# A two-layer encoder trunk on one core: the order of wide and narrow matmuls inside each projection

## The chip, the core and the metric

The kernel runs on one core of a Trainium2 chip. The core has five engines that run side by side, each through its own queue in order: TensorE (PE in the profile, with PEld for its weight loads), VectorE (DVE), ScalarE (ACT), GpSimd (POOL) and SyncE (SP), which here only issues DMA transfers. Engines wait for each other through semaphores. The metric is the device time of one execution in microseconds (us); before and after are compared by medians.

## The reference

An encoder of two residual layers over 256 tokens with 2048 features, batch 1, all in float32. Layer 0 mixes tokens by attention, layer 1 by a recurrence; each is followed by a gated feed-forward block with 5632 hidden features.

```
for i in range(2):
    h = rms_norm(x, norm_mix[i])
    mix = attention_mixer(h, ...) if i == 0 else recurrent_mixer(h, ...)
    x = x + mix
    h = rms_norm(x, norm_ffn[i])
    x = x + (silu(h @ w_gate) * (h @ w_up)) @ w_down
```

Attention has 16 query heads and 4 key and value heads of 128 features, a norm on queries and keys, and rotary positions. The recurrence has an input projection into two branches, a convolution of width four, gates, a forward and a backward scan, and an output projection. Almost all arithmetic is in the large projections.

## The kernel before, in words

Activations lie with features on the 128 partitions and the 256 tokens along the free dimension; 2048 features are 16 such tiles. Every large matrix is streamed once, in half chunks of eight (or six) blocks of 128 x 128 for one output tile. `load_half` (L83) fetches a half chunk with one DMA, ScalarE rounds it to the matmul's reduced format (`hi`, L93), and VectorE forms the remainder (`lo`, L94). Raw, hi and lo have five buffers each. The order in which half chunks are fetched is written out in advance (L114 to L121).

Activations are split in the same way: the first 256 columns of an activation tile hold the rounded values and the next 256 the remainders. A product is the sum of hi times both parts and lo times the rounded part; the product of the two remainders is left out. So each block of weights needs two matmuls in `blocks` (L153): hi against all 512 columns (L155), and lo against the first 256 (L156), accumulated into the second half of a PSUM tile `acc` of 512 columns. `evac` (L196) or `add_residual` (L279) later adds the halves of `acc`. There are four `acc` tiles.

`project` (L159) makes one output tile from two half chunks (16 blocks; 14 for some of the down projections). Feed-forward units, queries, values and most output tiles go through it. The keys call `blocks` with groups of four blocks (L329), and `output` (L178) calls it with whole half chunks, the first six blocks of one, and the last two. The recurrent layer's input projection, and the last output tile of each feed-forward block, use `project_sum` (L170) instead: three matmuls of 256 columns for each block, through `three` (L165).

The order of instructions on TensorE is that of the program. Small matmuls of other stages (scores, transposes, gates, norms) are inserted by hand: `later(delay, fn)` puts a stage on a list, and `step()` (L140), called once after every block, counts a clock and runs the oldest stage that is due. On the other engines a scheduler orders the instructions.

Of the kernel before, what the change touches and what calls it, by code (L numbers as in the profile page):

```python
# [19 lines left out]
S = 256  # L20
# [8 lines left out]
HALF = 8  # L29
# [30 lines left out]
def trunk(ctx, tc, w, out):  # L60
    nc = tc.nc
    act, dve, pool, pe, sync = nc.scalar, nc.vector, nc.gpsimd, nc.tensor, nc.sync
# [11 lines left out]
    def nm(s):  # L74
        uid[0] += 1
        return f"{s}_{uid[0]}"
# [47 lines left out]
    def half():  # L124
        n = taken[0]
        taken[0] += 1
        if n == 0:
            return load_half(*order[n], [partial(load_x, 2 * i, 2) for i in range(2)])
        if n < KT // 2 and n % 2 == 0:
            load_x(2 * n, 4)  # L130
        return load_half(*order[n])
# [8 lines left out]
    def step():  # L140
        clock[0] += 1
        due = [i for i, (t, _) in enumerate(waiting) if t <= clock[0]]
        if due:
            waiting.pop(due[0])[1]()
# [5 lines left out]
    def new_acc():  # L150
        return ps_a.tile([P, 2 * S], F32, tag="acc", name=nm("acc"))

    def blocks(acc, wt, xs, k0, total=KT):  # L153
        for k, (hi, lo) in enumerate(wt, k0):
            pe.matmul(acc, hi, xs[k], start=(k == 0), stop=False)  # L155
            pe.matmul(acc[:, S:], lo, xs[k][:, :S], start=False, stop=(k == total - 1))  # L156
            step()

    def project(xs):  # L159
        acc = new_acc()  # L160
        for k0 in range(0, len(xs), HALF):
            blocks(acc, half(), xs, k0, len(xs))
        return acc
# [14 lines left out]
    def output(xs, ready, norm, close):  # L178
        accs = [new_acc() for _ in range(FRONT)]
        for acc in accs:  # L180
            blocks(acc, half(), xs, 0)
        late = [half() for j in range(2)]
        for acc, wt in zip(accs, late):
            blocks(acc, wt[: ready - HALF], xs, HALF)
        flush()
        close()
        for j in range(KT):
            if j < 2:
                blocks(accs[j], late[j][ready - HALF :], xs, ready)
            elif j < FRONT:  # L190
                blocks(accs[j], half(), xs, HALF)
            acc = accs[j] if j < FRONT else project(xs)
            add_residual(j, acc, norm)
        norm.finish_later()
# [131 lines left out]
    for i in range(2 * KT // 4):  # L326
        wt = half()
# [397 lines left out]
```

## Time and profile before

| what | us |
|---|---|
| median of 3 executions | 2116.88 (2115.84 to 2120.38) |
| the profiled execution, its own time | 2129.33 |
| its span, first to last instruction | 2127.6 |
| TensorE busy within the span | 2085.5 |
| VectorE busy | 1502.9 |
| ScalarE busy | 1050.4 |
| GpSimd busy | 473.4 |

Busy times of engines overlap, so they don't add up. Matmuls are pipelined: the row of a matmul lasts from its start to a modelled end, and the next one starts well before that. The granted clock of TensorE averaged 0.993 of full speed. Lines are those of the kernel; one line can serve many places, as L155 and L156 serve all products that go through `blocks`.

### The profile page before, as it was taken

The numbers are of one execution on the slowest core, as the hardware profiler recorded it, in microseconds if no ns is written. First come the engines' busy times: TensorE is split into PE (matmuls) and PEld (weight loads), VectorE is DVE, ScalarE is ACT, GpSimd is POOL, SyncE is SP. The second block draws the span as 40 slices with busy tenths as digits, with TensorE's granted clock in tenths as the row PEclk, the third lists the DMA queues.
The fourth block names the chain that finished last, engine by engine and source line by source line (L and its number), as shares of the span: only waits on it lengthen the run. The fifth ranks groups of instructions, "written<-read, shape, count | busy, mean of one in ns | idle before, by whom it ended". The sixth has DMA issues, their size and how long they took to land.

```text
span 2127.6 us, 32676 instructions
## 1 busy us (share of the span) xinstructions
PE 2085.5 (98%) x12512; PEld 1848.4 (87%) x12512; DVE 1502.9 (71%) x2192; ACT 1050.4 (49%) x1598; POOL 473.4 (22%) x454
## 2 busy tenths in 40 slices
PE   7899999999999999999999998999999999999999
PEld 6788888888888888888999997888888888888888
DVE  8899876666566666668889898866666566666665
ACT  5465544443344434444587877454443444444442
POOL 5564431110011100113345553411110011001100
PEclk9999999999999999999999999999999999999999
DMA  6433655555555555555645454555555555665564
GB/s 239 146 122 118 203 187 189 185 185 186 187 188 188 173 186 195 188 183 177 196 160 169 161 166 157 185 188 190 190 194 189 189 189 187 183 203 190 188 189 138
DMA packets 112045, 384.27 MB, mean 181 GB/s; under 512 B 12560, under 2 KB 14736, under 8 KB 111888
## 3 DMA queue, kind: packets, MB, share of 16 engines
q1 hardware_dynamic: 111744, 382.17, 54.4%
q8 instruction: 98, 1.61, 0.3%
q14 instruction: 59, 0.48, 0.1%
q10 hardware_dynamic: 144, 0.02, 0.0%
HBM read 380.04 MB, written 2.10 MB: 180 GB/s over the span
## 4 chain that ended last, share of the span: by engine, by line
PE 86%; DVE 6%; issue 3%; ACT 2%; DMA 1%; POOL 1%; SPq 0%; ACTq 0%; DVEq 0%; POOLq 0%
PE acc L155 53%; PE acc L156 27%; DVE lo L94 2%; DMA graw<-in_w_gates_dram 1%; PE acc L168 1%; PE acc L167 1%; ACT sg L298 1%; PE acc L166 1%; PE pm L167 1%; POOL hb L351 1%; DVE xc L539 1%; PE pm L168 1%; DVE h L621 1%; ACT hi L93 1%; PE pm L166 1%
## 5 line engine op out<-in xcount | busy, mean ns | idle before, releaser
L94 DVE TENSOR_TENSOR lo<-raw,hi 128x1024 fp32r<-128x1024 f32 (+2 forms) x721 | 901.0, 1250 | 509.0 <-ACT hi L93 495.8
L93 ACT CAST hi<-raw 128x1024 fp32r<-128x1024 f32 (+2 forms) x721 | 740.8, 1029 | 928.2 <-PE acc L155 533.6
L155 PE MATMUL acc<-xg,hi 128*128 128x512 f32 x3200 | 1133.1, 398 | 5.7 <-ACT hi L93 5.7
L156 PE MATMUL acc<-xg,lo 128*128 128x256 f32 x3200 | 900.7, 281 | 5.4 <-DVE lo L94 5.4
L155 PEld LDWEIGHTS acc<-xg,hi 128*128 128x128 f32 x3200 | 603.4, 189 | 144.3 <-ACT hi L93 5.7
L155 PE MATMUL acc<-act,hi 128*128 128x512 f32 x1892 | 664.9, 396 | 4.6 <-DVE act L204 4.6
L156 PEld LDWEIGHTS acc<-xg,lo 128*128 128x128 f32 x3200 | 607.8, 190 | 7.1 <-DVE lo L94 7.0
L156 PE MATMUL acc<-act,lo 128*128 128x256 f32 x1892 | 530.9, 281 | 0.4 <-DVE lo L94 0.4
L155 PEld LDWEIGHTS acc<-act,hi 128*128 128x128 f32 x1892 | 355.8, 188 | 87.8 <-DVE act L204 5.5
L497 POOL TENSOR_TENSOR fg<-fg,nr 128x256 f32<-128x256 f32 x88 | 126.1, 1433 | 1189.9 <-ACT fg L298 1189.9
L156 PEld LDWEIGHTS acc<-act,lo 128*128 128x128 f32 x1892 | 358.4, 189 | 0.7 <-DVE lo L94 0.7
L168 PE MATMUL acc<-xg,lo 128*128 128x256 f32 x512 | 146.0, 285 | 3.0 <-DVE lo L94 3.0
L166 PE MATMUL acc<-xg,hi 128*128 128x256 f32 x512 | 146.4, 286 | 2.2 <-ACT hi L93 2.2
L167 PE MATMUL acc<-xg,hi 128*128 128x256 f32 x512 | 145.9, 285 | 0.0
L168 PEld LDWEIGHTS acc<-xg,lo 128*128 128x128 f32 x512 | 99.2, 194 | 3.8 <-DVE lo L94 3.8
L166 PEld LDWEIGHTS acc<-xg,hi 128*128 128x128 f32 x512 | 99.2, 194 | 3.1 <-ACT hi L93 3.1
L167 PEld LDWEIGHTS acc<-xg,hi 128*128 128x128 f32 x512 | 99.1, 194 | 0.0
L280 DVE TENSOR_TENSOR x<-x,acc 128x256 f32<-128x256 f32 x126 | 52.9, 420 | 57.8 <-PE acc L156 57.8
L254 POOL TENSOR_TENSOR ss<-ss,sq 128x256 f32<-128x256 f32 x60 | 78.1, 1302 | 4.9 <-ACT sq L250 0.7
L252 POOL TENSOR_TENSOR sq<-x 128x256 f32<-128x256 f32 x45 | 34.6, 769 | 114.6 <-DVE x L281 112.6
L244 DVE SCALAR_TENSOR_TENSOR xg<-x,pk,xg 128x256 fp32r<-128x256 f32 x64 | 56.2, 891 | 5.2 <-POOL xg L243 5.2
L351 POOL TENSOR_TENSOR hb<-hy,rope 32x256 f32<-32x256 f32 x60 | 46.1, 769 | 44.7 <-DVE hv L419 37.9
(164 smaller groups left out, 1486.6 us busy)
## 6 DMA issues: line engine op xcount, KB each, us to landing
raw<-in_w_gate_dram SPq DMA_DIRECT2D x176, 512.0 KB, 3.6
raw<-in_w_up_dram SPq DMA_DIRECT2D x176, 512.0 KB, 3.6
raw<-in_w_down_dram SPq DMA_DIRECT2D x128, 512.0 KB, 3.6
raw<-in_w_in_dram SPq DMA_DIRECT2D x64, 512.0 KB, 4.0
raw<-in_w_down_dram SPq DMA_DIRECT2D x64, 384.0 KB, 3.1
raw<-in_w_qv_dram SPq DMA_DIRECT2D x40, 512.0 KB, 3.7
raw<-in_w_o_dram SPq DMA_DIRECT2D x32, 512.0 KB, 3.6
raw<-in_w_out_dram SPq DMA_DIRECT2D x32, 512.0 KB, 3.7
```

Source lines behind the costliest of these rows:

```text
L93: act.copy(hi[:, sl, :], raw[:, sl, :])
L94: dve.tensor_tensor(lo[:, sl, :], raw[:, sl, :], hi[:, sl, :].bitcast(F32), ALU.subtract)
L155: pe.matmul(acc, hi, xs[k], start=(k == 0), stop=False)
L156: pe.matmul(acc[:, S:], lo, xs[k][:, :S], start=False, stop=(k == total - 1))
L166: pe.matmul(o, hi, x[:, :S], start=start, stop=False)
L167: pe.matmul(o, hi, x[:, S:], start=False, stop=False)
L168: pe.matmul(o, lo, x[:, :S], start=False, stop=stop)
L244: dve.scalar_tensor_tensor(t[:, S:], x_sb[k], g, t[:, :S].bitcast(F32), ALU.mult, ALU.subtract)
L254: pool.tensor_tensor(self.ss, self.ss, sq, ALU.add)
L280: dve.tensor_tensor(x_sb[j], x_sb[j], acc[:, :S], ALU.add)
L351: eng.tensor_tensor(b[32 * j : 32 * j + 32], y[32 * i : 32 * i + 32], s[32 * i : 32 * i + 32], ALU.mult)
L497: pool.tensor_tensor(g, g, norm.r, ALU.mult)
```

## The change

Within each call of `blocks`, the matmuls of 512 columns are no longer alternated with those of 256. All hi matmuls of the call are issued in a run, and all lo matmuls in another. Usually the hi run comes first. A call is turned, lo run first, if it is a later part of a product (`k0 >= HALF`), has more than four blocks, and the call before it was not turned. For a product of two half chunks this gives eight matmuls of 512, sixteen of 256 and eight of 512, and the next product begins with 512 again. `step()` is still called once per block: behind two of every three hi matmuls and one of every three lo matmuls. `stop` is set on whichever matmul is the last of its product. `three` and `project_sum` are as before.

```
-        for k, (hi, lo) in enumerate(wt, k0):
-            pe.matmul(acc, hi, xs[k], start=(k == 0), stop=False)
-            pe.matmul(acc[:, S:], lo, xs[k][:, :S], start=False, stop=(k == total - 1))
-            step()
+        def rounded():
+            for k, (hi, _) in enumerate(wt, k0):
+                pe.matmul(acc, hi, xs[k], start=(k == 0), stop=(k == total - 1 and turned))
+                if (k - k0) % 3 != 2:
+                    step()
+
+        def rest():
+            for k, (_, lo) in enumerate(wt, k0):
+                pe.matmul(acc[:, S:], lo, xs[k][:, :S], start=False, stop=(k == total - 1 and not turned))
+                if (k - k0) % 3 == 2:
+                    step()
+
+        turned = k0 >= HALF and narrow[0] and len(wt) > HALF // 2
+        narrow[0] = not turned
+        for part in (rest, rounded) if turned else (rounded, rest):
+            part()
```

More of the change, by code (lines that the diff above doesn't have):

```diff
@@ L151, in new_acc @@
         return ps_a.tile([P, 2 * S], F32, tag="acc", name=nm("acc"))
+    narrow = [True]
     def blocks(acc, wt, xs, k0, total=KT):
-        for k, (hi, lo) in enumerate(wt, k0):
-            pe.matmul(acc, hi, xs[k], start=(k == 0), stop=False)
-            pe.matmul(acc[:, S:], lo, xs[k][:, :S], start=False, stop=(k == total - 1))
-            step()
+        def rounded():
[12 more added lines that the diff above has]
+            part()
     def project(xs):
```

## The prediction

> **What bounds the kernel now.** I read the page first. TensorE is busy nearly all the time and carries the chain that ended last; two lines make up four fifths of that chain.
>
> ```profile
> span 2127.6 us, 32676 instructions
> PE 2085.5 (98%) x12512; PEld 1848.4 (87%) x12512; DVE 1502.9 (71%) x2192; ACT 1050.4 (49%) x1598; POOL 473.4 (22%) x454
> PE 86%; DVE 6%; issue 3%; ACT 2%; DMA 1%; POOL 1%; SPq 0%; ACTq 0%; DVEq 0%; POOLq 0%
> ...
> L155 PE MATMUL acc<-xg,hi 128*128 128x512 f32 x3200 | 1133.1, 398 | 5.7 <-ACT hi L93 5.7
> L156 PE MATMUL acc<-xg,lo 128*128 128x256 f32 x3200 | 900.7, 281 | 5.4 <-DVE lo L94 5.4
> ...
> L155 PE MATMUL acc<-act,hi 128*128 128x512 f32 x1892 | 664.9, 396 | 4.6 <-DVE act L204 4.6
> ...
> L156 PE MATMUL acc<-act,lo 128*128 128x256 f32 x1892 | 530.9, 281 | 0.4 <-DVE lo L94 0.4
> ```
>
> The change touches 3200 + 1892 = 5092 pairs of one 512-column and one 256-column matmul, and nothing else. The mean durations in these rows (398 and 281 ns) are no price: matmuls overlap, and what counts is the distance between starts. The idle time in front of the four groups is 16.1 us in all, so weights and activations are almost always there in time. So the question is what a pair costs when TensorE runs without a wait, and whether that price depends on the order.
>
> The price comes from the view by stretches, restricted to line 155, over two long stretches of feed-forward work, one in each layer.
>
> ```profile
> core 0: us, PE busy (x) PEld busy (x), PEclk, DMA share, GB/s
> 300.00:960.00 660.00, 659.20 (x1867) 350.57 (x1866) 1.00 0.56 186
> 1400.00:2050.00 650.00, 650.00 (x1876) 350.62 (x1875) 1.00 0.57 189
> ```
>
> Both stretches are full and at full granted clock, yet a pair takes 660.00/1867 = 353.5 ns in the first and 650.00/1876 = 346.5 ns in the second. The same code runs in two rhythms that differ by 7.0 ns a pair, and 1867 pairs at the slower one are 13.1 us of this execution. Weighted, the two stretches give 1310/3743 = 350.0 ns.
>
> The timeline shows how a pair divides in the fast rhythm:
>
> ```profile
> 1500.02 0.39 PE L155 MATMUL acc<-xg,hi 128*128 128x512 f32 x1
> 1500.25 0.28 PE L156 MATMUL acc<-xg,lo 128*128 128x256 f32 x1
> 1500.37 0.39 PE L155 MATMUL acc<-xg,hi 128*128 128x512 f32 x1
> 1500.60 0.28 PE L156 MATMUL acc<-xg,lo 128*128 128x256 f32 x1
> ```
>
> 0.23 us pass from a 512 to the 256 behind it, 0.12 us from a 256 to the 512. The recurrent layer gives the one neighbour that the change needs and that exists today, a 256 behind a 256 with a weight load before each:
>
> ```profile
> 1149.80 0.28 PE L167 MATMUL acc<-xg,hi 128*128 128x256 f32 x1
> 1149.92 0.28 PE L168 MATMUL acc<-xg,lo 128*128 128x256 f32 x1
> 1150.04 0.28 PE L166 MATMUL acc<-xg,hi 128*128 128x256 f32 x1
> ...
> 1150.64 0.28 PE L168 MATMUL acc<-xg,lo 128*128 128x256 f32 x1
> ```
>
> From 1149.80 to 1150.64 there are seven steps, so one is 120 ns. If a matmul's price depends on its own width alone, the 512 costs 346.5 - 120 = 226.5 ns. The difference of 106.5 ns for 256 columns is 0.416 ns a column, and both widths then leave the same rest: 120 - 106.5 = 13.5 ns, and 226.5 - 213.0 = 13.5 ns. That is what I take from the rows: a column price plus a fixed turn of 13.5 ns for each matmul with its weight load, whoever the neighbour is. It is an inference, since two prices always fit a line, but it asks for no cost of changing the width.
>
> **The change part by part.** It removes, adds and resizes no instruction. For each half chunk it issues eight 512s and eight 256s in runs; second halves of more than four blocks are turned, so that 256s meet 256s in the middle of a product and 512s meet 512s between products.
>
> First, the 256 behind a 256. It replaces the 0.12 us step that a 256 costs today; with the row of 120 ns and the division above this is 0 ns a pair.
>
> Second, the 512 behind a 512. No row of this trace has one. Its ends from the nearest rows are 213.0 ns (the column price with no turn at all) and 233.5 ns (the slow rhythm's pair of 353.5 less 120). I take 226.5, the fast rhythm's value, because the stretches of pure 256s show the turn of 13.5 ns without any change of width. In a stretch that is fast now that is a change of 0.
>
> At this term a rule of the Trainium skill speaks otherwise. TensorE: Matmul & The Clock Gate, section "Back-to-back issue gap", gives N/2.4 + 2.5 ns at full clock for an isolated stream; by it, as an estimate, a pair is 215.8 + 109.2 = 325 ns. This trace does not agree for alternating pairs (346.5) nor for pure 256s (120); whether it holds for a run of 512s no row shows.
>
> Third, the slow rhythm. Its steps are strictly regular, and its weight is 13.1 us in the first stretch. It appears only in the alternation of widths, and the order that carries it is gone. Whether runs of 512s have a slow rhythm of their own, and whether the unprofiled executions spend as long in it, no row tells: the gain lies between 0 and 13.1 us. I take the middle, 6.5 us. The profiled execution took 2129.33 us (span 2127.6 and 1.7 around it), 12.45 above the median of 2116.88; that distance could be this rhythm or the recording.
>
> Fourth, waits for weights. In a plain half only the rounded part is needed at first, and the remainder 8 x 226.5 = 1.81 us later. Such waits exist almost only at the beginning:
>
> ```profile
> 14.10 0.40 PE L155 MATMUL acc<-xg,hi 128*128 128x512 f32 x1
> 16.78 0.58 PE L156 MATMUL acc<-xg,lo 128*128 128x256 f32 x1 [2.29 <-DVE lo L94]
> ...
> 26.44 0.39 PE L155 MATMUL acc<-xg,hi 128*128 128x512 f32 x1
> 29.46 0.39 PE L156 MATMUL acc<-xg,lo 128*128 128x256 f32 x1 [2.63 <-DVE lo L94]
> ```
>
> At 26.44 seven more 512s (1.6 us) could run while TensorE waits for the remainder; at 14.10, in a group of four, three (0.7 us). The second wait lasts longer if the first is left earlier, so 1.6 us is the upper end. What is late next is the attention's chain over VectorE and GpSimd:
>
> ```profile
> PE pm L166 <- DVE qs L203: 4.7, 1, 4.7
> ...
> POOL hb L351 <- DVE hv L419: 37.9, 13, 5.6
> ```
>
> The scores wait 4.7 us for qs, later than both places, and that chain would swallow a head start. Between 0 and 1.6 I take 0.6 us. The lower end is not below nothing: no operand is needed earlier than now, except that a turned half wants its remainder 0.23 us sooner.
>
> Fifth, buffers. In a plain half the rounded weights are given back after 1.81 instead of about 2.65 us; in a turned half the remainders after 8 x 120 = 0.96 us. Only earlier, never later.
>
> ```profile
> ACT hi L93 <- PE acc L155: 533.6, 337, 3.7
> ...
> DVE lo L94 <- ACT hi L93: 495.8, 389, 4.6
> ```
>
> ScalarE waits 533.6 us for such a release, that is, the weights are already cast as far ahead as buffers allow. Earlier casts and the loads behind them collide with nothing on the chain. 0 us.
>
> Sixth, the steps that trigger the delayed stages. Eight calls a half stay eight, six in the run of 512s and two in that of 256s. In a plain half the sixth now comes after 1.81 instead of 2.08 us, 0.27 early; in a turned half the third comes after 0.96 + 0.23 = 1.19 instead of 1.04, 0.15 late. A stage that is inserted early makes TensorE stand in order behind its wait, with all later projections queued behind it. The 4.7 us wait could grow by 0.27, and a shift could remove or add a drop of the granted clock. I put this at 0, with 2 us to either side.
>
> The sum against the profiled execution is 2129.3 - 6.5 - 0.6 = 2122.2 us; the same 7.1 us from the median give 2109.8, so the forecast is **2110 us**. With the ends of the rhythm and the 2 us it reaches from 2101 to 2118.
>
> **The rivals.** *Runs of 512s are cheaper.* The turn may be a cost of the change of width rather than of each matmul. Against it stands the pure 256 stretch, which has no change of width and still pays 120. For it: there the weight load may be what fills the 120 ns, which says nothing about a 512. 512s meet 512s in 15 of 16 cases, 4774 times. With the whole turn gone this gives 4774 x 13.5 = 64 us, so 2052; with half of it gone, 32 us, so 2085. Chance 0.17. By the skill's rule (TensorE: Matmul & The Clock Gate, "Back-to-back issue gap") a 512 would be 215.8 ns, 51 us less and about 2066; the trace so far speaks against that rule for both widths that it shows.
>
> *Runs of 512s settle in the slow rhythm: slower.* In the slow stretch it is the pair with a 512 that lengthens, while the stretches of pure 256s hold 120. If a 512 behind a 512 takes 233.5 ns everywhere, a pair is 353.5 against 350.0 now: 5092 x 3.5 = 18 us more, 2135; if the unprofiled executions now run wholly in the fast rhythm, 5092 x 7.0 = 36 us, 2153. It decides from a pair above 350.8 ns on, where 0.8 ns x 5092 pass 4.2 us. Speaking against it: the slow rhythm is not met in every stretch today. Chance 0.24.
>
> *The order does not matter at all.* The share of each rhythm stays, or the unprofiled executions are fast already, and the beginning is swallowed by the attention's chain: 2116 to 2118. For it speaks that sum and count of instructions are the same. Chance 0.17.
>
> **How the numbers follow.** The forecast has the remaining 0.42. About 0.2% (4.2 us) can be told from no change. Of the forecast's case, from 2101 to 2118, 0.27 lie below 2112.7 and 0.15 above. Faster: 0.27 + 0.17 = 0.44. Same: 0.15 + 0.15 of the third rival = 0.30. Slower: 0.24 + 0.02 = 0.26. The range takes half of the first rival's span and half of the second's: 2085 to 2136, leaving out about 0.09 at each end. The likeliest case's own range is 2101 to 2118.
>
> **What would show it.** In the timeline of the second feed-forward block: 512 to 512 near 226 ns, 256 to 256 near 120 ns; 213 to 220 proves the first rival, 233 or more the second. In the two stretches: 346 to 347 ns a pair in both proves the third term, 353 in either one refutes it. In the first 30 us: the waits for the remainders shrink by about 1.6 us together, and the wait for qs grows by as much. A group of line 204 or 94 that suddenly holds TensorE for tens of microseconds, or more half-clock stretches in the attention, would make the prediction wrong for a reason that it does not name.

## The result, and the profile after

The changed kernel takes 2131.51 us (median of 4, 2128.63 to 2133.55) against 2117.71 us before (4 executions, three of them those shown above, 2115.84 to 2120.38): a ratio of 1.0063, with a 95% interval from 1.0046 to 1.0081. It is slower by 0.6%. Yet the two profiled executions are of the same length, 2127.6 us before and 2126.8 us after. Both facts have to be explained.

The page after shows TensorE with 12 us less busy time in the same span, and a chain that runs less over TensorE (81% against 86%) and more over VectorE and ScalarE:

```profile
PE 2073.5 (97%) x12512; PEld 1850.8 (87%) x12512; DVE 1519.5 (71%) x2192; ACT 1056.1 (50%) x1598; POOL 477.5 (22%) x454
...
PE 81%; DVE 9%; issue 3%; ACT 3%; POOL 2%; DMA 1%; SPq 0%; ACTq 0%; DVEq 0%; POOLq 0%
```

First the feed-forward work. Line 155 has become line 160, line 156 line 166. The view by stretches for line 160, with the same two stretches as before:

```profile
300.00:960.00 660.00, 451.94 (x1894) 347.96 (x1895) 1.00 0.58 188
1400.00:2050.00 650.00, 445.81 (x1869) 343.03 (x1868) 1.00 0.58 188
```

A pair takes 660.00/1894 = 348.5 ns in the first stretch and 650.00/1869 = 347.8 ns in the second. The slow rhythm of the first stretch (353.5) is gone, and the second (346.5) is 1.3 ns a pair dearer. The timeline shows the new order, eight 512s, sixteen 256s, and then 512s of two products:

```profile
1499.81 1.98 PE L160 MATMUL acc<-xg,hi 128*128 128x512 f32 x8
1501.63 2.08 PE L166 MATMUL acc<-xg,lo 128*128 128x256 f32 x16
1503.54 2.68 PE L160 MATMUL acc<-xg,hi 128*128 128x512 f32 x11
```

The last row is cut off by the end of the view.

Eight steps from 1499.81 to 1501.63 are 227.5 ns for a 512; sixteen from 1501.63 to 1503.54 are 119 ns for a 256. So far this is what was forecast, and worth 1894 x 5.0 = 9.5 us less in the first stretch and 1869 x 1.3 = 2.4 us more in the second.

What came back against it lies in the attention. The view by stretches from 100 to 200 us, before and then after; the counts are matmuls, weight loads, and instructions of VectorE, ScalarE and GpSimd:

```profile
100.00:200.00 100.00, 99.02 (x612) 85.61 (x611) 97.11 (x219) 61.23 (x185) 63.76 (x73) 1.00 0.38 127
```

```profile
100.00:200.00 100.00, 86.19 (x539) 73.05 (x538) 88.29 (x194) 53.38 (x164) 65.36 (x66) 1.00 0.32 111
```

TensorE starts 539 matmuls instead of 612. Before, VectorE was busy 97.11 of these 100 us and TensorE 99.02: here VectorE had almost no slack, although the page shows it at 71% of the whole span. After, VectorE and TensorE both have gaps. The wait view after names a wait that did not exist before, for the normalised softmax weights:

```profile
PE pm L454 <- DVE pr L448: 14.6, 24, 1.9
```

The copies of a head's projection out of PSUM mark the heads (first and last start in the stretch), before and after:

```profile
L198 ACT COPY hy<-acc x12: 358/364/371, 101.5 to 191.7; 128x256 f32<-128x256 f32 x12
```

```profile
L214 ACT COPY hy<-acc x10: 372/372/373, 109.0 to 191.7; 128x256 f32<-128x256 f32 x10
```

A head took 90.2/11 = 8.20 us before and takes 82.7/9 = 9.19 us after.

The two profiles can also be cut where TensorE starts the first 512-column matmul of a stage. The stretch of the sixteen query heads takes 134.0 us before and 146.0 after; the first feed-forward block together with the recurrence behind it 995.4 and 982.2; the second feed-forward block 728.6 and 730.7. So 12.0 us lost in the attention meet 13.2 us gained where the slow rhythm stood, and the two profiles are equally long. That the timed executions before had no slow rhythm to lose follows from the experiments.

Why, the queues of VectorE and ScalarE show. One head on VectorE before, then after (hv, rsq_s and hf work out a head's scale, mx its scaled maximum; pr are the softmax weights, here normalised, and qs is the split query):

```profile
136.97 0.15 DVE L419 SCALAR_TENSOR_TENSOR hv<-ms,ebt 128x2 f32<-128x2 f32 x1
...
137.63 0.32 DVE L274 TENSOR_TENSOR rsq_s<-hv,hf 128x2 f32<-128x2 f32 x1 [0.17 <-ACT hf L298]
...
139.54 0.16 DVE L423 TENSOR_TENSOR mx<-mx,hf 128x2 f32<-128x2 f32 x1
139.65 1.74 DVE L94 TENSOR_TENSOR lo<-raw,hi 128x1024 fp32r<-128x1024 f32 x1
...
142.11 1.12 DVE L432 TENSOR_SCALAR pr<-pr,rs 128x256 f32<-128x256 f32 x2
143.15 0.28 DVE L203 CAST qs<-hq 128x256 fp32r<-128x256 f32 x1
```

```profile
131.33 0.69 DVE L435 SCALAR_TENSOR_TENSOR hv<-ms,ebt 128x2 f32<-128x2 f32 x1
...
133.21 1.49 DVE L94 TENSOR_TENSOR lo<-raw,hi 128x1024 fp32r<-128x1024 f32 x1
134.63 0.69 DVE L290 TENSOR_TENSOR rsq_s<-hv,hf 128x2 f32<-128x2 f32 x1
135.33 0.29 DVE L219 CAST qs<-hq 128x256 fp32r<-128x256 f32 x1
...
136.79 0.15 DVE L439 TENSOR_TENSOR mx<-mx,hf 128x2 f32<-128x2 f32 x1
...
138.41 1.45 DVE L448 TENSOR_SCALAR pr<-pr,rs 128x256 f32<-128x256 f32 x2
```

Before, the remainder of a later half chunk (L94) and the split of the query (qs) stand behind the chain hv, rsq_s, mx; after, they stand inside it. From hv to mx it takes 2.57 us before and 5.46 us after. ScalarE's queue changed in two places. Before, then after:

```profile
139.74 0.56 ACT L298 ACTIVATE pr<-pm,mx,hf 128x256 f32<-128x256 f32 x1 [0.93 <-DVE mx L423]
...
141.89 0.37 ACT L198 COPY hy<-acc 128x256 f32<-128x256 f32 x1
```

```profile
131.19 1.05 ACT L93 CAST hi<-raw 128x1024 fp32r<-128x1024 f32 x1
132.13 0.21 ACT L314 ACTIVATE rsq_s<-hv 128x2 f32<-128x2 f32 x1
...
132.66 0.21 ACT L314 ACTIVATE hf<-rsq_s 128x2 f32<-128x2 f32 x1
136.36 0.37 ACT L214 COPY hy<-acc 128x256 f32<-128x256 f32 x1 [3.50 <-PE acc L160]
136.98 0.56 ACT L314 ACTIVATE pr<-pm,mx,hf 128x256 f32<-128x256 f32 x1 [0.24 <-DVE mx L439]
```

A weight cast runs ahead of rsq_s, and the exponential pr stands behind the copy of the next projection, which waits 3.50 us for TensorE. Before, the exponential stood ahead of that copy. Neither place costs much by itself in this head: rsq_s starts 0.11 us behind the end of hv (132.02), and the copy is over at 136.73, while the exponential waits another 0.24 us for mx; in every other head it starts right behind the copy, about 0.3 us after mx. The long delay is on VectorE: ScalarE's hf is over at 132.87, but VectorE's rsq_s, which needs it, starts at 134.63, as the remainder ahead of it ends. VectorE ran its queue in order here. The Trainium skill says the same (TensorE: Matmul & The Clock Gate, section "Architectural detail: the array is 16× 32×32, not 1× 128×128"): ScalarE and VectorE are strict first-in, first-out queues; these rows agree.

TensorE then waits in its own queue for pr, in the middle of a run, with all later projections behind it:

```profile
136.47 1.64 PE L160 MATMUL acc<-xg,hi 128*128 128x512 f32 x6
139.23 0.30 PE L454 MATMUL pm<-cn,pr 128*128 128x128 f32 x1 [1.12 <-DVE pr L448]
139.91 0.55 PE L454 MATMUL pm<-cn,pr 128*128 128x128 f32 x3 [0.38 <-DVE pr L448]
```

### The profile page after: what moved, and what is told of

Its sections match the earlier page's. It is cut to its first block, busy times and chain, and to the rows that moved or that the text cites. A ratio compares the mean times of both kernels' runs of the same rounds, so it can differ in the third digit from the quotient of the medians.

```text
span 2126.8 us, 32818 instructions
## 1 busy us (share of the span) xinstructions
PE 2073.5 (97%) x12512; PEld 1850.8 (87%) x12512; DVE 1519.5 (71%) x2192; ACT 1056.1 (50%) x1598; POOL 477.5 (22%) x454
## 4 chain that ended last, share of the span: by engine, by line
PE 81%; DVE 9%; issue 3%; ACT 3%; POOL 2%; DMA 1%; SPq 0%; ACTq 0%; DVEq 0%; POOLq 0%
PE acc L160 51%; PE acc L166 27%; DVE lo L94 3%; DMA graw<-in_w_gates_dram 1%; POOL hb L367 1%; ACT sg L314 1%; ACT pr L314 1%; DVE xc L555 1%; DVE h L637 1%; PE acc L182 1%; PE acc L183 1%; PE acc L184 1%; ACT L314 1%; DVE th L632 1%; DVE pr L448 1%
## 5 line engine op out<-in xcount | busy, mean ns | idle before, releaser
L94 DVE TENSOR_TENSOR lo<-raw,hi 128x1024 fp32r<-128x1024 f32 (+2 forms) x721 | 907.6, 1259 | 138.5 <-ACT hi L93 110.6
L93 ACT CAST hi<-raw 128x1024 fp32r<-128x1024 f32 (+2 forms) x721 | 741.3, 1030 | 435.4 <-PE acc L160 353.1
L160 PE MATMUL acc<-xg,hi 128*128 128x512 f32 x3200 | 780.9, 393 | 7.3 <-ACT hi L93 6.8
L160 PE MATMUL acc<-act,hi 128*128 128x512 f32 x1892 | 458.1, 392 | 5.1 <-DVE act L220 5.1
L166 PEld LDWEIGHTS acc<-xg,lo 128*128 128x128 f32 x3200 | 413.4, 192 | 19.7 <-DVE lo L94 4.0
L166 PE MATMUL acc<-xg,lo 128*128 128x256 f32 x3200 | 421.1, 284 | 2.7 <-DVE lo L94 2.7
L160 PEld LDWEIGHTS acc<-act,hi 128*128 128x128 f32 x1892 | 347.4, 189 | 71.4 <-DVE act L220 5.3
L166 PEld LDWEIGHTS acc<-act,lo 128*128 128x128 f32 x1892 | 246.1, 192 | 10.5
L166 PE MATMUL acc<-act,lo 128*128 128x256 f32 x1892 | 249.7, 283 | 0.0
L214 ACT COPY fg<-acc 128x256 f32<-128x256 f32 x88 | 32.9, 374 | 235.0 <-PE acc L160 235.0
L184 PE MATMUL acc<-xg,lo 128*128 128x256 f32 x512 | 145.8, 285 | 2.5 <-DVE lo L94 2.5
L214 ACT COPY fu<-acc 128x256 f32<-128x256 f32 x88 | 32.7, 372 | 231.6 <-PE acc L160 231.6
L182 PE MATMUL acc<-xg,hi 128*128 128x256 f32 x512 | 146.0, 285 | 1.2 <-ACT hi L93 1.2
L215 DVE TENSOR_TENSOR fu<-acc,fu 128x256 f32<-128x256 f32 x88 | 37.3, 424 | 146.4 <-ACT fu L214 146.4
L215 DVE TENSOR_TENSOR fg<-acc,fg 128x256 f32<-128x256 f32 x88 | 37.3, 424 | 134.2 <-ACT fg L214 134.1
L184 PEld LDWEIGHTS acc<-xg,lo 128*128 128x128 f32 x512 | 98.9, 193 | 3.3 <-DVE lo L94 3.3
```

Source lines behind the costliest of these rows:

```text
L93: act.copy(hi[:, sl, :], raw[:, sl, :])
L94: dve.tensor_tensor(lo[:, sl, :], raw[:, sl, :], hi[:, sl, :].bitcast(F32), ALU.subtract)
L160: pe.matmul(acc, hi, xs[k], start=(k == 0), stop=(k == total - 1 and turned))
L182: pe.matmul(o, hi, x[:, :S], start=start, stop=False)
L184: pe.matmul(o, lo, x[:, :S], start=False, stop=stop)
L214: act.copy(t, acc[:, S:])
```

## The experiments

The theories. **A**: the loss sits in the attention and comes from the order of the queues of ScalarE and VectorE. **B**: the kernel before is not always 2118 us long; something other than its rhythm (recording, transfers) makes its profiled execution longer. **C**: runs of 512s are dearer than alternation, everywhere. **D**: in the attention, the places of the inserted stages or the runs themselves make TensorE wait.

**The kernel before, again (e1).** No edit.

> The kernel before, unchanged, run and profiled once more. Theory A (the loss sits in the attention; the profiled execution before was long because of a slow rhythm of the alternating pairs, 353.5 instead of 346.5 ns a pair between 300 and 960 us): its own timed executions stay near 2117 us, and if this profile shows 346.5 ns a pair in both long stretches its span is near 2115 us; if it shows 353.5 in one, near 2127. Theory B (recording makes an execution of this kernel 12 us longer): the profiled execution is again near 2129 whatever the rhythm.

Twelve executions lay between 2114.90 and 2144.02 us, median 2132.36; A had expected them near 2117. All executions of the kernel before that were timed beside the experiments cluster at three levels, and the mix differs from session to session, also between the last two, which ran on the same chip:

| executions of the kernel before | to 2124 us | 2124 to 2136 | above 2136 |
|---|---|---|---|
| beside e1 to e4, 34 | 18 | 13 | 3 |
| beside e5 to e8, 31 | 8 | 12 | 11 |
| beside e9 to e12, 13 | 0 | 3 | 10 |
| beside e13 to e15, 25 | 23 | 2 | 0 |
| all, with 19 others, 122 | 55 | 36 | 31 |
| median of the level, us | 2118.5 | 2131.2 | 2142.5 |

Three single executions of it were profiled besides, for the other levels (e9, e10, e11).

> The kernel before once more, for one profiled execution. Executions so far lie at three levels, about 2118, 2131 and 2142 us. Rhythm theory: a pair takes 346.5 ns in both long stretches at the lowest level, 353.5 in one of them at the middle level, and 353.5 in both at the highest. Theory B (something other than the rhythm, such as transfers or the granted clock, sets the level): the levels do not follow these counts (1867 pairs between 300 and 960 us at 353.5, about 1905 at 346.5).

> A second look at the kernel before, for another of its levels; the same expectation: the time is the lowest level plus about 12.5 us for each feed-forward block whose pairs take 353.5 ns.

> A third look at the kernel before, for another of its levels; the same expectation of 12.5 us for each feed-forward block in the slow rhythm.

They took 2132.54, 2145.29 and 2141.30 us. Line 155 by stretches in the first and the second of them:

```profile
300.00:960.00 660.00, 658.64 (x1900) 355.36 (x1900) 1.00 0.58 189
1400.00:2050.00 650.00, 650.00 (x1841) 345.98 (x1840) 1.00 0.57 186
```

```profile
300.00:960.00 660.00, 659.19 (x1866) 350.46 (x1866) 1.00 0.57 186
1400.00:2050.00 650.00, 650.00 (x1841) 345.74 (x1840) 1.00 0.57 186
```

At 2132.54 us the first stretch is fast (660.00/1900 = 347.4 ns) and the second slow (650.00/1841 = 353.1); at 2145.29 and 2141.30 both are slow (1866 and 1869 pairs in the first, 1841 in the second). The profile before the change and that of e1 (2129.33 and 2129.74 us, 1867 and 1876 pairs in both) have the first slow and the second fast. Each feed-forward block falls into one of two rhythms, and each slow one costs 11 to 14 us: the levels lie 12.7 and 11.3 us apart, and the second block alone took 728.6 us in the profiles where it was fast and 742.5 where it was slow. The rhythm theory holds for the two upper levels. No profile caught this kernel at its lowest level; that both blocks are fast there follows from the steps, but was not seen. B in the form of a recording cost falls, since executions of the same kernel lie at every level.

**Runs in the feed-forward blocks alone (e2).** Elsewhere pairs alternate as before.

```
-        for k, (hi, lo) in enumerate(wt, k0):     # and the rest of the old body
+        (grouped if inside[0] else paired)(acc, wt, xs, k0, total)
```

> Runs of one width in the two feed-forward blocks alone; keys, queries, values and output projections alternate as before. Theory A (the loss sits in the attention): 2118 to 2122 us, that is the kernel before plus about 1 ns a pair on 4196 pairs; between 100 and 200 us TensorE starts about 612 matmuls as before. Theory C (runs of 512s are dearer than alternation, everywhere): near 2129 to 2131 us, since 82% of the pairs lie here.

2118.73 us (2116.90 to 2120.17, 12 executions, one level). Its attention is that of before:

```profile
100.00:200.00 100.00, 99.03 (x611) 85.42 (x609) 97.13 (x218) 61.23 (x185) 63.71 (x73) 1.00 0.38 127
```

C falls. In total, runs cost nothing that the lowest level of the kernel before doesn't cost too, and in these twelve executions they kept the kernel there, while 16 of the 34 executions of the kernel before beside them lay higher.

**Runs everywhere but there (e3).**

```
+        (grouped if not inside[0] else paired)(acc, wt, xs, k0, total)
```

> The converse: runs of one width everywhere but in the feed-forward blocks. Theory A: 2128 to 2131 us, with TensorE waiting for the softmax weights (pr) in the attention for some 14 us and about 540 matmuls started between 100 and 200 us. Theory C: 2117 to 2120 us.

2129.26 us (2127.14 to 2132.34, 12). The loss comes with the runs outside the feed-forward blocks; inside them its profile shows the fast rhythm twice (983.0 us for the first block with the recurrence, 728.6 for the second):

```profile
100.00:200.00 100.00, 86.20 (x536) 72.91 (x535) 88.29 (x195) 53.48 (x165) 65.32 (x66) 1.00 0.34 113
```

**Weights returned late (e4).** Seven 512s, seven 256s, then the last pair (turned: seven 256s first), with the stages called near their old times.

```
+        a, b = (r, w) if turned else (w, r)
+        seq = a[:-1] + b[:-1] + a[-1:] + b[-1:]
```

> Runs of seven 512s and seven 256s, and the last block of each half chunk as a pair at its end, so that both the rounded weights and the remainders of every half chunk are given back at its end, as before the change; the delayed stages are called as close as possible to their old times. Theory A in the form that the early return of the weights lets the casts of later half chunks move ahead of the softmax chain in the queues of ScalarE and VectorE: waits for pr vanish, 2117 to 2123 us. Theory D (the times at which stages are inserted, or long runs as such, make TensorE wait): near 2131 us if it is the runs; if it is only the insertion times this kernel is fast as well, and a kernel with the stages at their old times and the weights returned early tells the two apart.

2133.39 us (2131.37 to 2135.36, 11): not the range of A, and nearer to that of D. The remainder and the cast were back behind the softmax chain, and a head took 8.86 us; but VectorE had moved another instruction. The split of the query (qs) now stood ahead of the normalisation and waited there for GpSimd:

```profile
141.00 0.16 DVE L442 TENSOR_TENSOR mx<-mx,hf 128x2 f32<-128x2 f32 x1
141.11 1.74 DVE L94 TENSOR_TENSOR lo<-raw,hi 128x1024 fp32r<-128x1024 f32 x1
143.49 0.29 DVE L222 CAST qs<-hq 128x256 fp32r<-128x256 f32 x1 [0.63 <-POOL hq L372]
```

Besides, the extra changes of width cost in the feed-forward blocks, where this kernel started 1885 pairs in the first stretch (350.1 ns a pair). By stages, the heads took 140.1 us, so about half of their loss came back, and the first feed-forward block with the recurrence 5.6 us, the second 4.0 us more than in the changed kernel: the total hides what the attention regained. Theory A needed a test that sets the order of the queues directly.

**Queue order restored in part (e5).** The changed kernel, with ordering edges that add no semaphore (the comments are added here).

```
+            if second and p - 4 in heads:
+                behind(c, heads[p - 4]["hf"])     # cast behind the softmax factor
+                behind(d, heads[p - 4]["mx"])     # remainder behind the maximum
...
+        y = evac(acc, "hy", heads[h - 2]["pr"] ...)   # copy behind the exponential
```

> The changed kernel with ordering edges that cost no wait of their own: the cast of a later half chunk must stand behind the softmax factor and the probability copy in ScalarE's queue, its remainder behind the maximum in VectorE's, and the copy of the next head's projection behind the exponential. The query split still stands ahead of the normalisation. Theory A (the attention lost its time through the order of the two queues): most of it comes back, a head takes 8.3 to 8.9 us instead of 9.2, 2119 to 2126 us. Theory D (the runs or the places of the inserted stages make TensorE wait): still 2128 to 2132 us.

2127.16 us (2125.47 to 2127.97, 10), 8.90 us a head: a third of the loss came back, not most of it, and the time is 1.2 us above the range of A, though below that of D.

**Queue order restored (e6).** The query split is also emitted as a later stage, behind the normalisation of the head before.

```
+        def query():
+            behind(dve.tensor_copy(qs[:, :S], q), heads.get(h - 1, {}).get("nm"))
...
+            later(7, query)
```

> As the kernel with the edges, and the query split as a stage of its own behind the normalisation of the head before, so that VectorE's queue has the order that it had before the change. Theory A: a head takes 8.3 us again, waits for pr are gone, 2116 to 2121 us without any execution near 2130 or 2142, since runs have no slow rhythm. Theory D: 2128 to 2132 us.

2118.27 us (2117.86 to 2120.29, 10): A holds, D falls. The same matmuls in the same runs, with these queues close to the order of before, give back the loss. By the traces, TensorE's 12512 and GpSimd's 454 instructions stand in the same order as in the changed kernel, and VectorE and ScalarE run the same instructions in another order, all of it within the first 230 us; no wait for pr is left among TensorE's longer ones, and a head takes 91.8/11 = 8.35 us:

```profile
L230 ACT COPY hy<-acc x12: 363/366/370, 99.6 to 191.4; 128x256 f32<-128x256 f32 x12
```

In the totals, about 4.5 us of the loss belong to casts, remainders and the exponential, about 9 us to the query split once those stand right. The stretch of the heads alone went from 146.0 to 141.2 and to 135.6 us (133.9 in e14).

**Stages at their old times (e7).** The changed order of matmuls; stages called by elapsed matmul time.

```
+            spent += 227 if wide else 120
+            while done < n and spent + 60 >= 347 * (done + 1):
+                step()
```

> The changed order of matmuls, weights given back as early as in the changed kernel, but every delayed stage called as near as possible to its old time. Theory D (the times of the stages do it): 2117 to 2121 us. Theory A (the early return of weights changes the queues of ScalarE and VectorE): a head still takes more than 8.6 us, 2123 to 2131 us.

2138.63 us (2137.22 to 2139.78, 10), 9.92 us a head: slower than the changed kernel, and 7.6 us above the range of A. The matmuls of the values now waited 20.8 us for the transposed weights:

```profile
PE pm L185 <- DVE pT L460: 20.8, 14, 1.8
```

In this kernel the remainder again stood in the middle of the softmax chain, and in the one with weights returned late it did not. The two kernels differ only in the last pair of a half chunk, and the heads took 154.9 us here and 140.1 there, so it is the early return that moves it; which estimate of the scheduler does this was not looked into. D in the form of the times alone falls. The times matter all the same; that they act by shifting the queues too is likely, but no run shows it.

**Never turned (e8).** Every call 512s first.

```
-        turned = k0 >= HALF and narrow[0] and len(wt) > HALF // 2
+        turned = False
```

> Every call issues its 512s first and then its 256s: the changes of width double from two to four a product. If a change of width costs nothing but the few slower 512s behind it (227 to 235 ns instead of 227), a feed-forward pair stays at 348 to 349.5 ns. In the attention the remainders of second halves are returned later than in the changed kernel, and the order of VectorE's queue lies between the two: theory A expects 2120 to 2130 us and a head between 8.3 and 9.2 us.

2133.66 us (2132.82 to 2135.24, 10), 8.91 us a head, 660.00/1888 = 349.6 ns a pair in the first stretch. The pair is 1.1 ns dearer with twice as many changes of width; the total is 3.7 us above what A expected. By stages the heads took 139.9 us, 6.1 less than in the changed kernel, the first feed-forward block with the recurrence 5.9 us more and the second 2.8 us more: what A missed lies mostly outside the attention.

**Runs with restored order outside, alternation inside the feed-forward blocks (e12).**

```
+        (grouped if not inside[0] else paired)(acc, wt, xs, k0, total)   # on top of the restored order
```

> The runs of one width with the restored queue order outside the feed-forward blocks, and alternating pairs inside them. In the run with alternation only there, no execution of twelve showed the slow rhythm. If that holds: 346.7 ns a pair in both stretches against 348 of the runs, 4196 pairs, so 4 to 5 us below the kernel with the restored order, 2113 to 2116 us at one level. If the slow rhythm can return here: levels at about 2115, 2127 and 2139.

2142.58 us (2128.64 to 2144.08, 10), nine of them above 2140, with both stretches slow in its profile (1867 and 1841 pairs). The slow rhythm returns with the alternation; that twelve executions of e3 had not shown it was no protection. What decides the rhythm stays open.

**The changed kernel (e13), and that with the order restored (e14), in another session.** No edits.

> The changed kernel, unchanged. If runs of one width have no slow rhythm: 2128 to 2134 us whatever level the kernel before shows beside it, so slower than an execution of before at 2118, equal to one at 2131, faster than one at 2142. If the changed kernel has levels as well, they will show as steps of about 12 us.

> The changed kernel with the restored order of the queues, unchanged: 2117 to 2121 us at one level, about 12.5 us below the changed kernel on the same chip, as the share of the attention. If its 2118 us were a lucky level, it will show steps of about 12 us here.

2131.76 us (2129.61 to 2135.43, 10) and 2118.49 us (2116.14 to 2119.56, 10), beside 25 executions of the kernel before with a median of 2118.46. Neither has levels. The two differ by 13.3 us, which is the price of the queues. Against the kernel before, the changed one was slower by 0.6% again (ratio 1.0060, 1.0043 to 1.0077), since that kernel was at its lowest level in 23 of 25. That the changed kernel would beat an execution at 2142 follows from the levels, but the two were never timed side by side in such a session. The version with restored order was equal to the kernel before here (0.9999, 0.9983 to 1.0014) and faster beside e5 to e8, where the kernel before had a median of 2131.14 (0.9935, 0.9900 to 0.9970). It beats the changed kernel in every execution.

**Feed-forward pairs in twos (e15).** Two 512s, two 256s, and so on; elsewhere alternation.

> The kernel before with the feed-forward pairs in twos: two 512s, two 256s, and so on; all else alternates. If the slow rhythm needs strict alternation: one level, and a pair costs 346.7 ns plus what a change of width costs (of every two pairs one 512 follows a 256), 346.7 to 351. If any frequent change of width can carry it: levels as before, with 353 ns or more in one or both long stretches.

2123.32 us (2121.22 to 2125.58, 10), one level, 660.00/1894 = 348.5 ns a pair. In these ten the slow rhythm did not appear. That says little: the strictly alternating kernel beside them was at its lowest level in 23 of 25. Whether the slow rhythm needs strict alternation stays open.

## Why the prediction was wrong

The direction was wrong: 2110 us and faster were forecast, and 2131.5 us and slower by 0.6% came.

The step that failed is the fifth, buffers: "Earlier casts and the loads behind them collide with nothing on the chain. 0 us." A scheduler makes the order of ScalarE's and VectorE's queues. The matmul order, the return of buffers and the stages changed, and the queues came out in another order, with a weight cast, a remainder, a copy and a query split inside the softmax chain; e4 against e7 shows the early return as one source of it. That cost 13.3 us (e13 against e14). It was costed at nothing because the wait view showed ScalarE waiting 533.6 us for buffers; but only 1.6 us of them lie between 100 and 200 us, where VectorE had almost no room: 97.11 of 100 us busy. The prediction read no stretch of the attention. Of the 21.5 us between forecast and result, 13.3 are this step and 6.5 the gain of the third.

The sixth step, the stages, was sized at 0 with 2 us to either side. Placing them at their old times cost 6.9 us more (e7 against e13, from different sessions), outside those 2 us; through which mechanism, no run shows.

The first and the second step were right in kind. 119 ns for a 256 behind a 256 against 120; 227.5 ns for a 512 behind a 512 against 226.5. The constant turn of about 13 ns holds for runs, and the first rival falls. The rule of the Trainium skill (TensorE: Matmul & The Clock Gate, section "Back-to-back issue gap"), N/2.4 + 2.5 = 215.8 ns, does not agree with this run of 512s with a weight load before each; the page gives it for the isolated gap of a single matmul, not for such a stream.

The third step had the right mechanism: neither the 14 executions of the changed kernel nor the 42 of e2, e5, e6 and e14, which have the same runs in the feed-forward blocks, show a slow rhythm, and beside e2, e5 and e6 the kernel before lay above its lowest level in 39 of 65. Its size failed. The four executions before lay all at the lowest level, by chance, and there is nothing to gain there. The prediction had a sign of this: the profiled execution lay 12.45 us above the median, close to the 13.1 us of its one slow stretch. Its own test, 346 to 347 ns a pair in both stretches, gave 348.5 and 347.8, between its two answers; the second block with runs took 730.7 us against 728.6 in the fast alternation, 1.0 ns a pair more. The middle of 0 and 13.1 us was no likely value; with two blocks that can each be slow, the gain is 0, about 12 or about 25 us.

The fourth step came in part. The waits of these matmuls for remainders fell from 5.7 to 2.7 us, of which 1.1 came back as waits for rounded weights (5.7 to 6.8). The wait for qs did not grow by as much, as had been forecast (4.7 before, 4.9 after). It ended at 84.4 and 84.8 us in the profiles of the changed kernel and between 83.3 and 85.5 in the five of the kernel before, so a gain of 0.6 us can't be told from none:

```profile
PE acc L160 <- ACT hi L93: 6.8, 2, 5.8
...
PE pm L182 <- DVE qs L219: 4.9, 1, 4.9
...
PE acc L166 <- DVE lo L94: 2.7, 2, 2.3
```

That the second rival named a time close to the measured one (2135) is luck; its reason did not occur: a 512 in a run takes 227.5 and not 233.5 ns. (Its limit of 0.8 ns a pair gives 4.1 us and not 4.2; nothing hangs on it.) The note that a group of line 204 or 94 might hold TensorE for tens of microseconds was nearest to the cause, but it was given no price and no chance.

## What to carry to other kernels

Where a scheduler orders the other engines, a change on TensorE changes their queues too, even if it only gives buffers back earlier; look at the stretch where such an engine is nearly full, not at its share of the span, and compare the order of its queue around each chain. When one profiled execution stands well away from the median, look for two rhythms of the same code, and time the kernel before often enough to know its levels before a difference of half a per cent is believed. A quiet order (runs in the long blocks alone, or runs with the queue order held by edges) can be worth more than a fast one that is met only sometimes.

## What the runs showed of the hardware

The same sequence of instructions, a 512 and a 256 in turn with a weight load before each, ran at 346.5 or at 353.5 ns a pair at full granted clock, with the same count in every 100 us of a long stretch (284 pairs, or 289 to 290). One block of an execution could be slow and the other fast, and executions of the same kernel differed. With a weight load before each, the next matmul started 119 to 120 ns after a 256 and 226.5 to 227.5 ns after a 512, in runs as in the faster alternation; a price of N x 0.416 + 13.5 ns fits both, but two prices always fit a line.
